# Taking the mixing stage's arithmetic off GpSimd in a one-core decoder-layer kernel

## The chip, the core and the metric

The kernel runs as one program on one core of a Trainium2 chip. Five engines of that core work side by side, each through its own list of instructions, and wait for each other by semaphores: TensorE (PE; its weight loads are shown apart as PEld) multiplies matrices, VectorE (DVE) and ScalarE (ACT) do elementwise work, GpSimd (POOL) does elementwise work and starts some transfers, SyncE (SP) starts transfers. SBUF is the memory on the core that all of them read, PSUM the one that TensorE writes. The metric is the device time of one execution in microseconds (us). All inputs are float32.

## What is computed

One decoder layer on 512 tokens of width 1024, cut to what the kernel's stages are:

```
h = x + 1/2 * SwiGLU_1(RMSNorm(x))          # width 2816
z = RMSNorm(h) @ w_in                        # q | k,v cmp | k,v slc | k,v win | gates | u
q, kc, ksl, kw = rope(...)
o_nsa = nsa_attention(q, ...)                # 8 heads x 64, 2 groups of keys; three branches:
                                             # compressed, selected, window, summed by gates
o_s5  = s5_mixer(u, ...)                     # 32 groups x 16 channels, complex state of 64:
    x_t = a_bar * x_{t-1} + b * u_t          #   associative scan over the tokens
    y = gelu(Re(c x) + d u);  o_s5 = y * sigmoid(y @ w_glu + b_glu)
h = h + concat(o_nsa, o_s5) @ w_out
h = h + 1/2 * SwiGLU_2(RMSNorm(h))
h = h + sigmoid(RMSNorm(h) @ w_gate) * (p @ w_ple)
out = RMSNorm(h)
```

`compress` in the attention adds a position vector to each of the 32 tokens of a window (the "position sums" below), multiplies the flattened window by a matrix, applies gelu and multiplies again.

## The kernel before

Activations lie transposed: 128 features on the partitions, 512 tokens along the row, eight such blocks for width 1024. A product of float32 accuracy is made of three TensorE passes in the rounded type fp32r (`mm3`): the rounded weight `hi` times the rounded input, `hi` times the input's remainder, and the weight's remainder `lo` times the rounded input. Weights come in units of 128 x 1024 (`unit`, L129): one DMA into one of four `raw` buffers, started from ScalarE's queue; `hi` made by ScalarE (L142); `lo = raw - hi` (L143) made by VectorE, or by GpSimd where the caller passes `sub=G`. There are three buffers each of `hi` and `lo`.

The layer goes through FFN 1, the mixing stage (about 385 to 651 us of the profile, its first weight units some 20 us earlier), FFN 2, the embedding gate and the last norm. In the mixing stage:

- the projections (`proj`, L580) make keys, queries, S5 inputs `ut` and compressed keys. Rotated keys and queries and `ut` go out to DRAM and come back in another layout (`kd` and `kf`, `qd` and `qf`, `ud` and `u`, `kcd` and `cst`), by transfers that SyncE starts;
- `s5_all` works in eight chunks of four groups: TensorE makes the drive, VectorE turns it by a rotation (L638 to L641), scans (L644), and turns the state back: two products with the sine on half the partitions each (L647, L648, tile `t`), one with the cosine (L649), and their sum (L652, `xx`);
- `scores` prepares each block of 128 queries (`QA`, `QB`, L883 to L889; rows 64 to 111 of `QB` are zeroed and later hold shift rows, L964) and makes row maxima (L905) and exponentials (L593) of the scores;
- `windows` makes the position sums (L780), `cmp_all` the compressed keys and values with a gelu between its two products, `glu` the S5 outputs: gelu (L596 to L602), a product, a tanh, `sg` (L846), and the split of the result into `oh` and `ol` (L849, L850);
- `out_half` adds the half of the output projection that takes the S5 outputs, column block by column block (L864), and the values of the attention follow, with the other half at the end.

A scheduler sets the order of the instructions on each engine from the program's text and its own estimate of the times; `weave` interleaves the S5 chunks, the scores and the remaining projections in the text. Each engine then works strictly in its order: an instruction that waits holds everything behind it on its engine.

Of the kernel before, what the change touches and what calls it, by code (L numbers as in the profile page):

```python
# [10 lines left out]
F32 = mybir.dt.float32  # L11
# [65 lines left out]
def block_kernel(ctx: ExitStack, tc: tile.TileContext, a: dict, out: bass.AP):  # L77
# [48 lines left out]

    unit_i = [0]

    def unit(raw_only=False, keep=None, sub=None, q=nc.scalar):  # L129
        i = unit_i[0]  # L130
        unit_i[0] += 1
        w = UNIT_W[i]
        if i not in raws:
            load_unit(i, q)
        raw = raws.pop(i)
        if raw_only:
            return raw
        pool, n = (keep, 5) if keep else (ring, 3)
        hi = pool.tile([128, UNIT], FR, tag="hi", name="hi", bufs=n)
        lo = pool.tile([128, UNIT], FR, tag="lo", name="lo", bufs=n)  # L140
        for c in ((slice(0, 512), slice(512, w)) if i == 0 else (slice(0, w),)):
            S.copy(hi[:, c], raw[:, c])  # L142
            (sub or V).tensor_tensor(lo[:, c], raw[:, c], hi[:, c].bitcast(F32), OP.subtract)  # L143
        return hi, lo

    def mm3(o, wh, wl, xh, xl, first, last):
# [391 lines left out]
    def mixer(ctx):  # L538
# [39 lines left out]
        V.tensor_copy(KBc[0:64], zero[0:64, 0:1].to_broadcast([64, 160]))  # L578

        def proj(tag="A"):  # L580
            wu = unit(sub=G)
            o = bank(tag)
            for k in range(KT):
                sl = slice(k * 128, (k + 1) * 128)
                mm3(o, wu[0][:, sl], wu[1][:, sl], nm.xh[:, k, :], nm.xl[:, k, :], k == 0, k == KT - 1)
            return o
# [8 lines left out]
        def gelu2(o, x, w, tag):  # L595

            t = tp.tile([128, SEQ], F32, tag=tag, name="gt")[:, :w]
            act(t, x, AF.Square)
            G.tensor_scalar(t, t, 0.044715, 1.0, OP.mult, OP.add)
            V.tensor_tensor(t, t, x, OP.mult)  # L600
            act(t, t, AF.Tanh, scale=math.sqrt(2 / math.pi))
            V.scalar_tensor_tensor(o, t, 1.0, x, OP.add, OP.mult)  # L602


# [25 lines left out]
        def s5_in(j):  # L630
            sc = s5w.tile([128, GC, 512], F32, tag="sc", name="sc", bufs=3)
            G.dma_start(sc, s5d[:, GC * j:GC * j + GC])
            co, si = sc[:, :, 384:448], sc[:, :, 448:512]
            w = bank(TW, (128, GC, 64))
            for g in range(GC):
                mm(w[:, g], sc[:, g, 0:128], u8[:, GC * j + g], True, True)
            t1, t2 = (s5w.tile([128, GC, 64], F32, tag=n, name=n) for n in ("t1", "t2"))
            V.tensor_tensor(t1, w, co, OP.mult)  # L638
            V.tensor_tensor(t2[64:128], w[0:64], si[0:64], OP.mult)
            V.tensor_tensor(t2[0:64], w[64:128], si[64:128], OP.mult)  # L640
            V.tensor_tensor(t1, t1, t2, OP.subtract)  # L641
            vv = s5w.tile([128, GC, 64], F32, tag="vv", name="vv", bufs=1)
            for g in range(GC):
                V.tensor_tensor_scan(vv[:, g], r8[:, GC * j + g:GC * j + g + 1].to_broadcast([128, 64]), t1[:, g],  # L644
                                     0.0, OP.mult, OP.add)
            x1, x2 = (s5w.tile([128, GC, 64], F32, tag=n, name=n) for n in ("t1", "t2"))
            G.tensor_tensor(x2[64:128], vv[0:64], si[0:64], OP.mult)  # L647
            G.tensor_tensor(x2[0:64], vv[64:128], si[64:128], OP.mult)  # L648
            V.tensor_tensor(x1, vv, co, OP.mult)  # L649
            xx = s5w.tile([128, GC, 64], F32, tag="xx", name="xx")  # L650
            G.memset(xx[:, :, 0:1], 0.0)
            V.tensor_tensor(xx[:, :, 1:64], x1[:, :, 0:63], x2[:, :, 0:63], OP.add)  # L652
            return sc, xx
# [90 lines left out]


        def v_gates():
            wv = [unit(sub=G) for _ in range(3)]
            for b in range(4):
                o = bank("A")
                ov = o[:, :280]  # L750
                for k in range(KT):
                    wt = wv[k // 3]
                    sl = slice((k % 3) * 280, (k % 3) * 280 + 280)
                    xs = slice(b * 128, (b + 1) * 128)
                    mm(ov, nm.xh[:, k, xs], wt[0][:, sl], k == 0, False)
                    mm(ov, nm.xh[:, k, xs], wt[1][:, sl], False, False)
                    mm(ov, nm.xl[:, k, xs], wt[0][:, sl], False, k == KT - 1)
                r1 = nm.ri[:, b:b + 1]
                pv = o[:, 0:256].rearrange("p (r d) -> p r d", r=4)
                S.activation(VL[:, b, :, 0:64], pv, AF.Copy, scale=r1)  # L760
                V.scalar_tensor_tensor(VL[:, b, :, 64:128], pv, r1, VL[:, b, :, 0:64].bitcast(F32),
                                       OP.mult, OP.subtract)
                V.tensor_scalar(gp1[:, b], o[:, 256:280], r1, -1.0, OP.mult, OP.mult)
                yield
            act(gp1, gp1, AF.Exp)
            V.tensor_scalar(gp1, gp1, 5e35, 1.0, OP.min, OP.add)


        def windows(src, i, dst):
            ev = []  # L770
            for g in range(2):
                st = tp.tile([128, SEQ], F32, tag=f"r{g + 1}", name="cst")
                nc.sync.dma_start(st[0:64], src[:, g])
                nc.sync.dma_start(st[64:128, 0:SEQ - 1], src[:, g, 1:SEQ])
                ev.append(st.rearrange("p (j l r) -> p l j r", l=8, r=2)[:, :, :, 0])
            sp = []
            for half, t in enumerate(dst):
                t = t.rearrange("p (l g j) -> p l g j", l=8, g=2)
                for g in range(2):
                    G.tensor_tensor(t[:, :, g], ev[g],  # L780
                                    pe[:, i, 8 * half:8 * half + 8, None].to_broadcast([128, 8, 32]), OP.add)
                sp.append(t)
            return sp
# [42 lines left out]
        def glu():  # L826

            for m in range(4):
                yt = yts[m]
                gelu2(yt, yt, SEQ, ("r1", "r2")[m % 2])  # L830
                S.activation(oh[:, m], yt, AF.Copy, scale=0.5)
                V.scalar_tensor_tensor(ol[:, m], yt, 0.5, oh[:, m].bitcast(F32), OP.mult, OP.subtract)
            yield
            for m in range(4):
                if m % 2 == 0:
                    wu = unit(sub=G)
                o = bank("A")
                for k in range(4):
                    q = (m * 4 + k) % 8
                    sl = slice(q * 128, (q + 1) * 128)  # L840
                    mm3(o, wu[0][:, sl], wu[1][:, sl], oh[:, k], ol[:, k], k == 0, k == 3)
                sg = mp.tile([128, 8, 64], F32, tag="ut", name="sg", bufs=2)
                act(sg.rearrange("p t c -> p (t c)"), o, AF.Tanh, scale=0.5, bias=bglu[:, m:m + 1])
                yf = mp.tile([128, 8, 64], F32, tag="ra", name="yf", bufs=2)
                G.tensor_tensor(yf.rearrange("p t c -> p (t c)"), oh[:, m].bitcast(F32), ol[:, m].bitcast(F32), OP.add)
                V.scalar_tensor_tensor(sg, sg, 1.0, yf, OP.add, OP.mult)  # L846
                nat = sg.rearrange("p t c -> p c t")
                hv_ = oh[:, 4 + m].rearrange("p (c t) -> p c t", t=8)
                S.activation(hv_, nat, AF.Copy, scale=0.5)  # L849
                V.scalar_tensor_tensor(ol[:, 4 + m].rearrange("p (c t) -> p c t", t=8), nat, 0.5, hv_.bitcast(F32),  # L850
                                       OP.mult, OP.subtract)
                yield

        def out_half(ks, done=None, sub=None):
            n = len(ks)
            for m in range(KT):
                o = bank("A")
                for j, k in enumerate(ks):
                    q = (m * n + j) % 8
                    if q == 0:  # L860
                        wu = unit(sub=sub)
                    sl = slice(q * 128, (q + 1) * 128)
                    mm3(o, wu[0][:, sl], wu[1][:, sl], oh[:, k], ol[:, k], j == 0, j == n - 1)
                V.tensor_tensor(h[:, m], h[:, m], o, OP.add)  # L864
# [7 lines left out]
        def scores(qb, env, pool, tags="B", stage=("ra", "ra")):  # L872
# [5 lines left out]
            for hs, st in zip((slice(0, 4), slice(4, 8)), stage):  # L878
                if st == "ra":
                    qf = mp.tile([128, 4, 128], F32, tag=st, name="qf", bufs=2)  # L880
                else:
# [4 lines left out]
                V.tensor_scalar(QB[0:64, hs], qf[0:64], 0.125, None, OP.mult)  # L886
                V.scalar_tensor_tensor(QA[64:128, hs], qf[64:128], 0.125, QA[64:128, hs].bitcast(F32),
                                       OP.mult, OP.subtract)
            G.tensor_copy(QB[64:112].rearrange("p h q -> p (h q)"), zero[64:112, 0:1].to_broadcast([48, 1024]))  # L889
            env.update(QA=QA, QB=QB)  # L890
            yield

# [160 lines left out]
        drain(cg)  # L1053
        drain(gg)
        cc = tp.tile([128, SEQ], FR, tag="rb1", name="cc")[:, :192].rearrange("p (q a c) -> p q a c", q=4, a=2)
        fill = out_half(range(4, 8), sub=G)
        drain(compressed(3, 2))
        shifts(2, 4)
        sg = chain(s1, compressed(1), s0, compressed(0))
# [254 lines left out]
```

## Time and profile before

| | before |
|---|---|
| median of 3 runs | 1113.75 us (1112.89 to 1115.28) |
| profiled execution | 1112.43 us, of which span 1110.6 us |
| PE busy | 1063.3 us, 96% |
| DVE busy | 670.7 us, 60% |
| ACT busy | 389.0 us, 35% |
| POOL busy | 246.5 us, 22% |
| chain that ended last | PE 83%, DVE 5%, DMA 5% |

Busy times are unions, so overlapping ends of one engine's instructions count once. The chain of waits is followed back from the last instruction; what is on it set the end. In the windows view a stretch of the span is taken by itself: the busy time of each engine in it, with the count of instructions, the clock that TensorE was granted there (1.00 is 2.4 GHz, 0.5 is 1.2 GHz) and the DMA engines' share. In the views of waits, an engine's idle time is put down to what came last among the things it waited for.

### The profile page before, as it was taken

To read this page: it belongs to the slowest core of one execution; us is meant where nothing else is said; L and a number is where in the kernel's file an instruction comes from. 1 tells how busy PE (TensorE), PEld (TensorE's weight loads), DVE (VectorE), ACT (ScalarE), POOL (GpSimd) and SP (SyncE) were. 2 spreads that over 40 slices of the span, in tenths; PEclk is the share of its full clock that TensorE was granted. 3 is DMA by queue.
4 is the path that set the end of the run, shared out by engine and by line. 5 is a ranking of instruction groups with operands and counts; after the bars stand their busy time and mean duration, and the time that the engine had idled before them with its cause. 6 is when DMAs were issued, how large, how long until landed. Compare 5 with 4: busy or idle time off the path is not lost.

```text
span 1110.6 us, 13320 instructions
## 1 busy us (share of the span) xinstructions
PE 1063.3 (96%) x5134; PEld 865.4 (78%) x5134; DVE 670.7 (60%) x1129; ACT 389.0 (35%) x636; POOL 246.5 (22%) x245
## 2 busy tenths in 40 slices
PE   7999999999999998898889999999999999999995
PEld 5888888888888886676667578888888888888795
DVE  6995446445448645587777975644454445356755
ACT  6222222123123413256648864221222222224631
POOL 4006146335538533455300000000000000000000
PEclk9999999999999999998899999999999999999998
DMA  7332225327625736667011003233333322232402
GB/s 254 111 114 95 95 95 152 114 95 163 173 101 146 247 114 170 188 203 236 23 58 39 1 21 96 92 105 95 104 95 95 95 95 94 96 95 95 132 1 76
DMA packets 46283, 124.16 MB, mean 112 GB/s; under 512 B 10044, under 2 KB 16796, under 8 KB 45196
## 3 DMA queue, kind: packets, MB, share of 16 engines
q10 hardware_dynamic: 26352, 91.04, 25.4%
q0 software_dynamic: 4336, 17.60, 6.1%
q1 hardware_dynamic: 15532, 14.68, 4.5%
q8 instruction: 40, 0.66, 0.2%
q14 instruction: 23, 0.19, 0.0%
HBM read 109.90 MB, written 13.63 MB: 111 GB/s over the span
## 4 chain that ended last, share of the span: by engine, by line
PE 83%; DVE 5%; DMA 5%; issue 3%; ACT 2%; SPq 1%; POOL 0%; POOLq 0%; DVEq 0%; ACTq 0%
PE ps_A L124 29%; PE ps_B L124 26%; PE ps_C L124 25%; PE ps_D L124 3%; DMA kf<-kd 1%; DMA kd<-r 1%; DMA kcd<-ra 1%; DMA qd<-r 1%; DVE nmax L905 1%; ACT e L593 1%; DVE ol L850 0%; ACT eh L593 0%; ACT ps_B L593 0%; DVE sg L846 0%; DMA raw<-in_wpack 0%
## 5 line engine op out<-in xcount | busy, mean ns | idle before, releaser
L142 ACT CAST hi<-raw 128x1024 fp32r<-128x1024 f32 (+2 forms) x168 | 174.9, 1043 | 540.8 <-PE ps_C L124 184.4
L143 DVE TENSOR_TENSOR lo<-raw,hi 128x1024 fp32r<-128x1024 f32 (+1 forms) x147 | 191.1, 1303 | 75.3 <-ACT hi L142 75.0
L124 PE MATMUL ps_A<-xh,hi 128*128 128x512 f32 (+1 forms) x448 | 170.3, 380 | 7.8 <-ACT xh L164 6.7
L124 PE MATMUL ps_A<-xl,hi 128*128 128x512 f32 (+1 forms) x448 | 169.7, 379 | 0.1
L124 PE MATMUL ps_A<-xh,lo 128*128 128x512 f32 (+1 forms) x448 | 168.9, 377 | 0.8 <-DVE lo L143 0.8
L124 PE MATMUL ps_B<-xh,lo 128*128 128x512 f32 (+1 forms) x432 | 161.9, 375 | 1.2 <-POOL lo L143 1.2
L124 PE MATMUL ps_B<-xl,hi 128*128 128x512 f32 (+1 forms) x432 | 161.8, 374 | 0.0
L124 PE MATMUL ps_B<-xh,hi 128*128 128x512 f32 (+1 forms) x432 | 161.4, 374 | 0.0
L124 PE MATMUL ps_C<-hh,hi 128*128 128x512 f32 x352 | 136.9, 390 | 0.7 <-DVE h L254 0.7
L124 PE MATMUL ps_C<-hl,hi 128*128 128x512 f32 x352 | 137.0, 389 | 0.0
L124 PE MATMUL ps_C<-hh,lo 128*128 128x512 f32 x352 | 136.9, 389 | 0.0
L193 POOL TENSOR_TENSOR ri<-ms,negh 128x4 f32<-128x4 f32 (+1 forms) x6 | 6.5, 1077 | 540.3 <-DVE ms L192 540.3
L124 PEld LDWEIGHTS ps_A<-xh,hi 128*128 128x128 f32 x448 | 85.3, 190 | 24.0 <-ACT xh L164 6.7
L124 PEld LDWEIGHTS ps_A<-xl,hi 128*128 128x128 f32 x448 | 85.3, 190 | 16.6 <-DVE xl L165 1.3
L124 PEld LDWEIGHTS ps_A<-xh,lo 128*128 128x128 f32 x448 | 85.4, 191 | 16.3 <-DVE lo L143 1.0
L232 DVE TENSOR_TENSOR t<-ps_B,rb 128x512 f32<-128x512 f32 x42 | 29.0, 690 | 111.9 <-PE ps_B L124 111.7
L124 PEld LDWEIGHTS ps_B<-xh,lo 128*128 128x128 f32 x432 | 81.1, 188 | 16.4 <-POOL lo L143 1.7
L124 PEld LDWEIGHTS ps_B<-xl,hi 128*128 128x128 f32 x432 | 81.2, 188 | 14.7 <-issue 0.2
L124 PEld LDWEIGHTS ps_B<-xh,hi 128*128 128x128 f32 x432 | 81.2, 188 | 14.5 <-issue 0.2
L254 DVE SCALAR_TENSOR_TENSOR h<-ps_C,h 128x512 f32<-128x512 f32 x64 | 43.9, 689 | 67.0 <-PE ps_C L124 66.9
L124 PEld LDWEIGHTS ps_C<-hh,hi 128*128 128x128 f32 x352 | 66.1, 188 | 15.2 <-DVE h L254 1.5
L124 PEld LDWEIGHTS ps_C<-hh,lo 128*128 128x128 f32 x352 | 66.1, 188 | 13.7
(361 smaller groups left out, 1664.4 us busy)
## 6 DMA issues: line engine op xcount, KB each, us to landing
raw<-in_wpack ACTq DMA_DIRECT2D x168, 512.0 KB, 3.6
sc<-s5d POOLq DMA_DIRECT2D x8, 1024.0 KB, 6.6
raw<-in_wpack SPq DMA_DIRECT2D x4, 512.0 KB, 8.3
h<-in_xT SPq DMA_DIRECT2D x8, 256.0 KB, 4.8
s5d<-fs POOLq DMA_DIRECT2D x1, 2048.0 KB, 11.8
s5d<-gt POOLq DMA_DIRECT2D x1, 2048.0 KB, 12.5
s5d<-tcs POOLq DMA_DIRECT2D x2, 1024.0 KB, 9.5
qf<-qd SPq DMA_DIRECT2D x16, 128.0 KB, 3.7
```

What stands on the lines that cost most here:

```text
L124: PE.matmul(o, lhsT, rhs, start=start, stop=stop, **kw)
L142: S.copy(hi[:, c], raw[:, c])
L143: (sub or V).tensor_tensor(lo[:, c], raw[:, c], hi[:, c].bitcast(F32), OP.subtract)
L193: G.tensor_tensor(ri, ms, negh[:, :nb], OP.pow)
L232: V.tensor_tensor(t3, z[1], nrm.rb, OP.mult)
L254: V.scalar_tensor_tensor(h[:, m, :], o, 0.5, h[:, m, :], OP.mult, OP.add)
L593: S.activation(*args, **kw)
L905: V.tensor_reduce(mc, s_, AX.X, OP.max, negate=True)
```

## The change

No instruction of the mixing stage computes on GpSimd any longer, apart from its memsets, a scaling of a 128 x 4 tile and the power in the norm. Six edits:

1. 21 `lo` subtractions (18 of 1024 columns, two of 840, one of 560) go from GpSimd to VectorE; the `sub` argument is gone.
2. The two sine products of each of the eight S5 chunks (L647, L648, 64 x 256) go to VectorE.
3. The eight position sums (L780, 128 x 256) go to VectorE.
4. The four zeroings of `QB`'s rows (L889, 48 x 1024) go to ScalarE.
5. gelu's middle: the GpSimd operation `t = 0.044715 t + 1` and the VectorE product by `x` become one VectorE operation, `(t + 1/0.044715) x`, with the factor moved into the tanh's scale. Five times.
6. glu: the sum `yf = oh + ol` on GpSimd (L845, four times) is gone; `sg` is multiplied by `yts[m]`, which is twice that sum, and the factor 0.5 becomes 0.25. The tile `sg` takes the buffers ("ra") that `yf` had.

```diff
--- before.py
+++ after.py
@@ -126,7 +126,7 @@
-    def unit(raw_only=False, keep=None, sub=None, q=nc.scalar):
+    def unit(raw_only=False, keep=None, q=nc.scalar):
@@ -140,7 +140,7 @@
             S.copy(hi[:, c], raw[:, c])
-            (sub or V).tensor_tensor(lo[:, c], raw[:, c], hi[:, c].bitcast(F32), OP.subtract)
+            V.tensor_tensor(lo[:, c], raw[:, c], hi[:, c].bitcast(F32), OP.subtract)
         return hi, lo
@@ -578,7 +578,7 @@
-            wu = unit(sub=G)
+            wu = unit()
@@ -596,9 +596,8 @@
             act(t, x, AF.Square)
-            G.tensor_scalar(t, t, 0.044715, 1.0, OP.mult, OP.add)
-            V.tensor_tensor(t, t, x, OP.mult)
-            act(t, t, AF.Tanh, scale=math.sqrt(2 / math.pi))
+            V.scalar_tensor_tensor(t, t, 1 / 0.044715, x, OP.add, OP.mult)
+            act(t, t, AF.Tanh, scale=math.sqrt(2 / math.pi) * 0.044715)
             V.scalar_tensor_tensor(o, t, 1.0, x, OP.add, OP.mult)
@@ -644,8 +643,8 @@
             x1, x2 = (s5w.tile([128, GC, 64], F32, tag=n, name=n) for n in ("t1", "t2"))
-            G.tensor_tensor(x2[64:128], vv[0:64], si[0:64], OP.mult)
-            G.tensor_tensor(x2[0:64], vv[64:128], si[64:128], OP.mult)
+            V.tensor_tensor(x2[64:128], vv[0:64], si[0:64], OP.mult)
+            V.tensor_tensor(x2[0:64], vv[64:128], si[64:128], OP.mult)
             V.tensor_tensor(x1, vv, co, OP.mult)
@@ -777,7 +776,7 @@
                 for g in range(2):
-                    G.tensor_tensor(t[:, :, g], ev[g],
+                    V.tensor_tensor(t[:, :, g], ev[g],
                                     pe[:, i, 8 * half:8 * half + 8, None].to_broadcast([128, 8, 32]), OP.add)
@@ -833,32 +832,31 @@
                 if m % 2 == 0:
-                    wu = unit(sub=G)
+                    wu = unit()
                 o = bank("A")
...
                     mm3(o, wu[0][:, sl], wu[1][:, sl], oh[:, k], ol[:, k], k == 0, k == 3)
-                sg = mp.tile([128, 8, 64], F32, tag="ut", name="sg", bufs=2)
+                sg = mp.tile([128, 8, 64], F32, tag="ra", name="sg", bufs=2)
                 act(sg.rearrange("p t c -> p (t c)"), o, AF.Tanh, scale=0.5, bias=bglu[:, m:m + 1])
-                yf = mp.tile([128, 8, 64], F32, tag="ra", name="yf", bufs=2)
-                G.tensor_tensor(yf.rearrange("p t c -> p (t c)"), oh[:, m].bitcast(F32), ol[:, m].bitcast(F32), OP.add)
+                yf = yts[m].rearrange("p (t c) -> p t c", t=8)
                 V.scalar_tensor_tensor(sg, sg, 1.0, yf, OP.add, OP.mult)
...
                 hv_ = oh[:, 4 + m].rearrange("p (c t) -> p c t", t=8)
-                S.activation(hv_, nat, AF.Copy, scale=0.5)
-                V.scalar_tensor_tensor(ol[:, 4 + m].rearrange("p (c t) -> p c t", t=8), nat, 0.5, hv_.bitcast(F32),
+                S.activation(hv_, nat, AF.Copy, scale=0.25)
+                V.scalar_tensor_tensor(ol[:, 4 + m].rearrange("p (c t) -> p c t", t=8), nat, 0.25, hv_.bitcast(F32),
                                        OP.mult, OP.subtract)
...
 
-        def out_half(ks, done=None, sub=None):
+        def out_half(ks, done=None):
             n = len(ks)
...
                     if q == 0:
-                        wu = unit(sub=sub)
+                        wu = unit()
                     sl = slice(q * 128, (q + 1) * 128)
@@ -886,7 +884,7 @@
                                        OP.mult, OP.subtract)
-            G.tensor_copy(QB[64:112].rearrange("p h q -> p (h q)"), zero[64:112, 0:1].to_broadcast([48, 1024]))
+            S.copy(QB[64:112].rearrange("p h q -> p (h q)"), zero[64:112, 0:1].to_broadcast([48, 1024]))
             env.update(QA=QA, QB=QB)
@@ -1053,7 +1051,7 @@
         cc = tp.tile([128, SEQ], FR, tag="rb1", name="cc")[:, :192].rearrange("p (q a c) -> p q a c", q=4, a=2)
-        fill = out_half(range(4, 8), sub=G)
+        fill = out_half(range(4, 8))
         drain(compressed(3, 2))
```

The three units of `v_gates` (L747) lose their `sub=G` in the same way.

The scheduler reorders around this. Line numbers after the change are one or two lower. The places follow at which the order matters most; tile names carry the number of their buffer.

The first place is VectorE in the projections, in the order before: `ut` are the S5 inputs, `KB` the remainders of the keys that came back from DRAM.

```order
L609 TENSOR_TENSOR ut_3282<-ps_A_3257,rb_3110 128x64x8
L609 TENSOR_TENSOR ut_3316<-ps_D_3291,rb_3110 128x64x8
L722 TENSOR_TENSOR KB_3009<-kf_3157,KA_3008 64x512
L722 TENSOR_TENSOR KB_3009<-kf_3162,KA_3008 64x512
L609 TENSOR_TENSOR ut_3358<-ps_A_3333,rb_3110 128x64x8
L722 TENSOR_TENSOR KB_3009<-kf_3167,KA_3008 64x512
L722 TENSOR_TENSOR KB_3009<-kf_3172,KA_3008 64x512
L609 TENSOR_TENSOR ut_3392<-ps_D_3367,rb_3110 128x64x8
L705 TENSOR_TENSOR r1_3465<-ps_B_3409,cosr_3048 128x512
L706 TENSOR_TENSOR r2_3467<-ps_B_3409,sinr_3049 128x512
```

In the order after the change, the same stretch:

```order
L608 TENSOR_TENSOR ut_3282<-ps_A_3257,rb_3110 128x64x8
L608 TENSOR_TENSOR ut_3316<-ps_D_3291,rb_3110 128x64x8
L143 TENSOR_TENSOR lo_3406<-raw_3403,hi_3405 128x1024
L721 TENSOR_TENSOR KB_3009<-kf_3157,KA_3008 64x512
L721 TENSOR_TENSOR KB_3009<-kf_3162,KA_3008 64x512
L608 TENSOR_TENSOR ut_3358<-ps_A_3333,rb_3110 128x64x8
L143 TENSOR_TENSOR lo_3437<-raw_3434,hi_3436 128x1024
L721 TENSOR_TENSOR KB_3009<-kf_3167,KA_3008 64x512
L721 TENSOR_TENSOR KB_3009<-kf_3172,KA_3008 64x512
L608 TENSOR_TENSOR ut_3392<-ps_D_3367,rb_3110 128x64x8
L143 TENSOR_TENSOR lo_3522<-raw_3519,hi_3521 128x1024
L704 TENSOR_TENSOR r1_3465<-ps_B_3409,cosr_3048 128x512
```

The subtractions `lo_3406` to `lo_3630`, which had GpSimd's order to themselves, now stand between these; `lo_3437` stands behind `ut_3358`.

The second place is VectorE where the shift rows are written into `QB_3505`, the first of the blocks of queries whose values follow, in the order before: `h_66` is the residual, to which each column block of the output projection (`ps_A`) is added.

```order
L905 TENSOR_REDUCE nmax_3055<-ps_B_4702 128x2
L864 TENSOR_TENSOR h_66<-h_66,ps_A_5195 128x512
L143 TENSOR_TENSOR lo_5549<-raw_5546,hi_5548 128x1024
L905 TENSOR_REDUCE nmax_3055<-ps_B_4723 128x2
L964 TENSOR_TENSOR QB_3505<-ps_D_4578,sel_3023 48x1024
L864 TENSOR_TENSOR h_66<-h_66,ps_A_5341 128x512
L905 TENSOR_REDUCE nmax_3055<-ps_B_4757 128x2
```

After the change:

```order
L862 TENSOR_TENSOR h_66<-h_66,ps_A_5478 128x512
L903 TENSOR_REDUCE nmax_3055<-ps_B_4710 128x2
L143 TENSOR_TENSOR lo_5581<-raw_5578,hi_5580 128x1024
L903 TENSOR_REDUCE nmax_3055<-ps_B_4744 128x2
L962 TENSOR_TENSOR QB_3505<-ps_D_4565,sel_3023 48x1024
L862 TENSOR_TENSOR h_66<-h_66,ps_A_5492 128x512
L903 TENSOR_REDUCE nmax_3055<-ps_B_4799 128x2
L862 TENSOR_TENSOR h_66<-h_66,ps_A_5512 128x512
L143 TENSOR_TENSOR lo_5625<-raw_5622,hi_5624 128x1024
L903 TENSOR_REDUCE nmax_3055<-ps_B_4831 128x2
```

In the order before, four additions to `h_66` stand ahead of `QB_3505` in all, and in the order after it six; all but two of the first half's eight are done by then.

The third place is ScalarE around the block of queries `QA_4325` and the compressed keys `KAc`, in the order before; lines L593 are exponentials of scores (`ps_B`) and the tanh and squares of gelu (`gt`).

```order
L885 ACTIVATE QA_4325<-qf_4327 128x512
L885 ACTIVATE QA_4325<-qf_4333 128x512
L806 ACTIVATE chid_4397<-ps_C_4394 128x256
L593 ACTIVATE gt_4379<-yt_4234 128x512
L593 ACTIVATE ps_B_4038,den_3056<-ps_B_4038,nmax_3055 128x384
L106 DMA raw_5546<-in_wpack 128x1024
L814 CAST KAc_3012<-ps_D_4399 64x2x31
L815 CAST KAc_3012<-ps_D_4399 64x2x31
L822 CAST VLc_3011<-ps_D_4406 31x64
L593 ACTIVATE ps_B_4072,den_3056<-ps_B_4072,nmax_3055 128x384
```

After the change:

```order
L883 ACTIVATE QA_4325<-qf_4327 128x512
L883 ACTIVATE QA_4325<-qf_4333 128x512
L887 CAST QB_4326<-zero_3036 48x1024
L593 ACTIVATE ps_B_4100,den_3056<-ps_B_4100,nmax_3055 128x384
L887 CAST QB_4341<-zero_3036 48x1024
L813 CAST KAc_3012<-ps_D_4394 64x2x31
L814 CAST KAc_3012<-ps_D_4394 64x2x31
L593 ACTIVATE gt_4376<-yt_4234 128x512
```

The two zeroings of `QB_4326` and `QB_4341` stand in between now.

## Rows read from the trace of the kernel before

**Rows 1.** Windows: busy of PE, PEld, DVE, ACT, POOL; clock; DMA share; GB/s.

```profile
360.00:385.00 25.00, 25.00 (x112) 20.71 (x111) 18.80 (x25) 11.35 (x16) 12.67 (x15) 1.00 0.87 281
...
515.00:540.00 25.00, 18.91 (x82) 12.71 (x81) 18.74 (x30) 15.96 (x45) 10.36 (x7) 0.75 0.34 107
...
577.00:651.00 74.00, 69.70 (x325) 48.21 (x324) 62.13 (x127) 59.95 (x146) 0.00 (x0) 1.00 0.06 20
...
464.80:576.80 112.00, 97.63 (x602) 72.94 (x602) 90.31 (x179) 62.17 (x150) 47.65 (x49) 0.91 0.43 138
```

**Rows 2.** Waits of TensorE, 416 to 577 us: total us, times, longest.

```profile
PE ps_A L124 <- DVE h L864: 4.2, 1, 4.2
...
PE ps_C L124 <- DMA ud<-ut: 4.1, 1, 4.1
...
PE ps_B L124 <- ACT ps_B L593: 3.4, 5, 1.2
...
PE ps_C L804 <- DVE ht L602: 2.0, 1, 2.0
...
PE ps_B L124 <- POOL lo L143: 1.2, 1, 1.2
```

**Rows 3.** The timeline, GpSimd and VectorE near 561 us: start, length, engine, line.

```profile
560.94 2.34 POOL L143 TENSOR_TENSOR lo<-raw,hi 128x1024 fp32r<-128x1024 f32 x1 [5.22 <-ACT hi L142]
...
561.09 2.23 DVE L943 TENSOR_SCALAR lw<-lw 128x48 int32<-128x48 int32 x1
```

**Rows 4.** Groups of VectorE, 464.8 to 576.8 us: busy us, mean ns, idle.

```profile
L850 DVE SCALAR_TENSOR_TENSOR ol<-sg,oh 128x512 fp32r<-128x512 f32 x4 | 6.6, 1649 | 1.1 <-ACT oh L849 1.1
...
L602 DVE SCALAR_TENSOR_TENSOR yt<-gt,yt 128x512 f32<-128x512 f32 x4 | 5.1, 1283 | 0.0
...
L846 DVE SCALAR_TENSOR_TENSOR sg<-sg,yf 128x512 f32<-128x512 f32 x4 | 4.8, 1198 | 2.3 <-ACT sg L593 2.3
...
L886 DVE TENSOR_SCALAR QB<-qf 64x512 fp32r<-64x512 f32 x5 | 4.5, 921 | 1.7 <-DMA qf<-qd 1.7
...
L832 DVE SCALAR_TENSOR_TENSOR ol<-yt,oh 128x512 fp32r<-128x512 f32 x4 | 4.1, 1034 | 0.3 <-ACT oh L831 0.3
...
L649 DVE TENSOR_TENSOR t<-vv,sc 128x256 f32<-128x256 f32 x7 | 3.1, 443 | 0.0
...
L143 DVE TENSOR_TENSOR lo<-raw,hi 128x1024 fp32r<-128x1024 f32 x1 | 1.2, 1218 | 0.0
```

**Rows 5.** Source view of three such lines: shortest, median, longest ns.

```profile
L850 DVE SCALAR_TENSOR_TENSOR ol<-sg,oh x4: 1069/1159/3209, 544.9 to 557.4; 128x512 fp32r<-128x512 f32 x4
...
L886 DVE TENSOR_SCALAR QB<-qf x5: 408/419/2118, 471.6 to 530.4; 64x512 fp32r<-64x512 f32 x5
...
L832 DVE SCALAR_TENSOR_TENSOR ol<-yt,oh x4: 667/688/2094, 499.5 to 537.9; 128x512 fp32r<-128x512 f32 x4
```

**Rows 6.** The waits of VectorE from 464.8 to 576.8 us.

```profile
DVE nmax L905 <- PE ps_B L124: 7.7, 7, 3.6
...
DVE xx L652 <- POOL t L648: 2.7, 2, 2.1
...
DVE h L864 <- PE ps_A L124: 1.9, 1, 1.9
...
DVE gt L600 <- POOL gt L599: 1.0, 2, 0.5
```

**Rows 7.** The page's fifth part, the cast on ScalarE.

```profile
L142 ACT CAST hi<-raw 128x1024 fp32r<-128x1024 f32 (+2 forms) x168 | 174.9, 1043 | 540.8 <-PE ps_C L124 184.4
```

**Rows 8.** The timeline, VectorE and TensorE, from 431 to 440 us.

```profile
431.06 1.09 DVE L609 TENSOR_TENSOR ut<-ps_A,rb 128x512 f32<-128x512 f32 x1 [6.23 <-DMA ud<-ut]
...
434.17 1.06 DVE L609 TENSOR_TENSOR ut<-ps_D,rb 128x512 f32<-128x512 f32 x1
...
434.72 0.39 PE L124 MATMUL ps_B<-xh,lo 128*128 128x512 f32 x1
...
439.16 1.94 PE L124 MATMUL ps_C<-u,sc 128*128 128x64 f32 x8 [4.05 <-DMA ud<-ut]
```

More of the change, by code (lines that the diff above doesn't have):

```diff
@@ L746, in v_gates @@
         def v_gates():
-            wv = [unit(sub=G) for _ in range(3)]
+            wv = [unit() for _ in range(3)]
             for b in range(4):
```

## Prediction

> **What bounds the kernel now.** I read the page first: TensorE is 96% busy and most of the chain that set the end. So only TensorE's idle time, and time at a lower clock, can be won. The windows view shows where that is [rows 1]. In 360 to 385 us TensorE is busy without a gap while VectorE has 18.80 of 25 us of work and GpSimd 12.67. From 464.8 us (the first score maxima) to 576.8 (the shift rows go into `QB_3505`) it is busy 97.63 of 112.0 us at a granted clock of 0.91, so about 14.4 us idle and some more at the half clock (0.75 in 515 to 540). After that, to 651 us, GpSimd does nothing; TensorE is busy 69.70 of 74.00 us, VectorE 62.13, ScalarE 59.95.
>
> TensorE's waits in 416 to 577 us come next [rows 2]: 4.2 us for one addition to the residual on VectorE, 4.1 for the S5 inputs' way through DRAM, 3.4 for ScalarE's exponentials in five pieces, 2.0 for gelu's last operation on VectorE; of those put down to GpSimd's `lo` the larger is 1.2. So GpSimd is hardly waited for directly. The timeline shows how it matters all the same [rows 3]: at 561.09 VectorE's operation on a 128x48 tile takes 2.23 us and ends 0.04 us after GpSimd's `lo` (560.94, 2.34 us). The lines of such a group have ordinary and very long members, 667 to 2094 ns at L832, 408 to 2118 at L886, 1069 to 3209 at L850 [rows 5], the long ones beside GpSimd's operations. So GpSimd's work costs VectorE time, and VectorE is what TensorE waits for.
>
> **The change part by part.** The sum is made in four stretches, against the profiled execution of 1112.43 us.
>
> *To 416 us: 0.* Three of the `lo` move between FFN 1's last operations on VectorE, 3 x 1.22 [rows 4] = 3.7 us, where 6.2 us of 25 are idle and TensorE has no gap [rows 1]; that idle time is the cover. Without it they cost at most these 3.7. A zeroing of `QB` on ScalarE (nearest: the cast of 128x1024, 1.04 us [rows 7]) lies beside 13.65 us of idle time there.
>
> *416 to 464.8 us: +0.4.* Seven subtractions leave GpSimd (2.34 us for one of 1024 columns [rows 3]) and take 1.22 on VectorE [rows 4], but stand in its order now. `lo_3437` is behind `ut_3358`, which VectorE could start only at 431.06, for a transfer, and which takes 1.09 [rows 8]. So it runs from about 432.1 to 433.3. It is used in the third of 24 matmuls whose last started at 434.72; at one in 25.00/112 = 0.223 us [rows 1] the third was due at 430.0, and is due at 428.8 once the 1.2 us for `lo_3406` [rows 2] is not lost: a new wait of 4.5. Its 21 remaining steps of 0.223 us end at about 438.4. In the trace TensorE stood still there until 439.16, for the S5 inputs [rows 8], so the new wait lies within the old one of 1.2 and the 4.1 us. What counts is the transfer: it starts with `ut_3392` (434.17), which has `lo_3437` and two `KB` of 0.6 ahead of it (KB and `ut` both queue behind the waiting instruction) and starts at about 434.6: +0.4. Bounds: -2.3 (if what VectorE loses today beside GpSimd at its `KB` starts all transfers earlier by as much), and +3 (if two more subtractions of 1.22 get ahead of `ut_3392` and the new wait outlasts the old).
>
> *464.8 to 576.8 us: -1.7.* VectorE's 90.31 us there hold time in which it only stood still. Each line's count times what its mean is above its shortest: L850 4 x 0.58, L602 4 x 0.60 (the shortest as at L832, 0.68), L846 4 x 0.52, L886 5 x 0.51, L832 4 x 0.37, and 2.0 at L943 for an operation that I take at 0.2: 12.8 us [rows 3 to 5]. This goes. What comes, at durations of the same stretch [rows 4]: 14 sine products (0.44, as 128x256 at L649) 6.2, eight position sums (0.44) 3.5, seven `lo` 8.5 and the narrow one 0.7, and, since they stand ahead of `QB_3505` now, two residual additions and one maximum of 128x512 (0.68 each) 2.0: 20.9. So 90.3 - 12.8 + 20.9 = 98.4 us of work. The folded gelu costs VectorE nothing, one operation for one. Before, VectorE idled 21.7 us. The waits for GpSimd go (2.7 + 1.0); so do the one for the addition (1.9) and about half of the longest for TensorE (3.6 [rows 6]), which followed the 2.0 us wait for gelu; and added work fills some 2 us of the rest. That leaves 12: 110.4 us in place of 112.0, or, with rounding, -1.7. Bounds: VectorE 95% busy (103.5 us, -8.5), or idle as long as before (120.1, +8.1). I take a value nearer to the low idle, since more work in the same queue fills gaps. The two zeroings on ScalarE near 520 us stand ahead of exponentials that TensorE waits for; ScalarE is busy only 15.96 of 25 us there [rows 1], so I take 0, bound 2 x 1.04 = +2.1.
>
> By the Trainium skill, Perfetto Trace Analysis, section "Optimizing Scalar/DVE Operations", work may be offloaded from a saturated VectorE to ScalarE or even GpSimd, with the doubt that the shared port may leave nothing won between VectorE and GpSimd. By its first half this change goes the wrong way, as VectorE comes to 98.4 of some 110 us (89%); by its second half the 12.8 us are the price of the offloading. The rows bear out the second half (12.8 us lost on VectorE for 20.9 us saved there) and also the first, as a balance of 8 us is left against the change.
>
> *576.8 to 651 us: -3.3.* At `QB_3505` TensorE has done two more column blocks of the output projection, 24 matmuls at 0.223 us, 5.4, and a small group of scores: some 6 us less is left for the stretch after. With TensorE at 94% there, nearly all of it would count; with VectorE at 84% and ScalarE at 81% as second and third limit I take little more than half. Bounds: 0 and -6.
>
> The removal of `yf` shortens a chain on GpSimd that VectorE had no long wait for: 0, covered by VectorE's other work.
>
> Sum: 0 + 0.4 - 1.7 - 3.3 = -4.6, so 1112.43 becomes 1107.8. The profiled execution lies 1.3 us under the median of the runs shown; put on top, this gives 1109.1: I predict 1109.
>
> **The rivals.** *A, VectorE becomes the bound.* Between 464.8 and 576.8 us VectorE keeps its old idle time, because its operations stand in a fixed order among the waits for TensorE's scores, for ScalarE and for transfers, and each `lo` now stands behind one of these, with TensorE waiting for the `lo`. It decides from an idle time of 16.5 us on: 98.4 + 16.5 = 114.9 is +2.9, which uses up the 0.4 - 3.3 of the other stretches. At 21.7 us of idle it is +8.1, in all +5.2: 1119. For it: VectorE's busiest stretch gets busier, and TensorE's longest waits [rows 2] are for VectorE, not GpSimd. Against it: 3.7 of the 21.7 us were waits for GpSimd itself.
>
> *B, the stalls go altogether.* VectorE at 95% (-8.5), the front -2.3, the last stretch -6: -16.8, so 1097. For it: TensorE's idle time and half clock in the middle hold more than that [rows 1], and the waits for the addition and for gelu's end (4.2, 2.0) follow held-up operations. Against: 3.4 us of waits are for ScalarE, and the transfers stay.
>
> *C, no change.* The round trips through DRAM hold the front, and what VectorE gains by not standing still it spends on the new work: within 2 us, 1112 to 1116. For it: 12.8 against 20.9 us, close to a balance after the idle time.
>
> **How the numbers follow.** Forecast 0.42, A 0.28, B 0.13, C 0.17. The range is 1099 to 1120; it takes in A's point and most of B's, and leaves out A's and B's ends. The forecast's own range is 1105 to 1113, by half of its bounds on either side. About 0.2%, or 2.2 us, is what a measurement of this kernel can tell from no change. Of the forecast 0.37 lies more than that under 1113.75 and 0.05 within; with B that is 0.50 faster. C and a little of A (0.04) make it 0.26 within. The rest of A, 0.24, is slower.
>
> **What would show it.** Right: no VectorE operation of 128x512 over 1.3 us in 416 to 577; VectorE's busy time from its first score maximum to `QB_3505` near 98 us and its stretch near 110; a wait of TensorE of 4 to 5 us for a VectorE `lo` near 429; the wait of 4.2 for the addition gone or under 2; the stretch after `QB_3505` some 3 us shorter. Wrong: waits of TensorE for VectorE's `lo` or maxima of over 10 us in all in the middle (A); VectorE without gaps there and the clock near 1.00 (B); the late operations on VectorE as long as before, which would mean that not GpSimd held them up.

## The result, and the profile after

| | before | after |
|---|---|---|
| median | 1114.85 us, 8 runs | 1108.61 us, 8 runs |
| profiled span | 1110.6 us | 1104.2 us |
| PE busy | 1063.3 us | 1059.0 us |
| DVE busy | 670.7 us | 681.7 us |
| ACT busy | 389.0 us | 393.4 us |
| POOL busy | 246.5 us | 164.4 us |

The ratio of after to before is 0.9934, 95% interval 0.9913 to 0.9955: 0.66% faster, 6.2 us by the medians. The forecast was 1109, from a sum of -4.6 us; the spans of the profiled executions differ by 6.4. Of these 6.4 us, 4.3 are TensorE's busy time, for the same 5134 matmuls, and 2.1 its idle time (47.3 to 45.2). The windows view of after, its middle stretch bounded by the same instructions as in [rows 1]:

```profile
360.00:385.00 25.00, 25.00 (x112) 20.71 (x111) 18.67 (x28) 12.40 (x17) 4.62 (x11) 1.00 0.82 279
...
515.00:540.00 25.00, 17.29 (x88) 11.18 (x86) 19.02 (x44) 16.31 (x42) 0.00 (x0) 0.71 0.14 42
...
463.80:578.20 114.40, 102.75 (x637) 77.25 (x637) 96.98 (x216) 66.59 (x157) 2.67 (x9) 0.91 0.41 138
...
578.20:650.80 72.60, 69.16 (x321) 47.88 (x320) 61.80 (x128) 59.08 (x144) 0.00 (x0) 1.00 0.04 14
```

The middle (from the product `ra`, L740, just ahead of the first score maxima, to the end of the write into `QB_3505`) takes 114.4 us, 2.4 more than before, and TensorE does 637 matmuls in it in place of 602. The stretch behind it takes 72.6 us up to the end of the first addition of the last half's column blocks. In before that stretch was 79.6 us long:

```profile
576.80:656.40 79.60, 75.30 (x350) 52.58 (x348) 64.56 (x132) 60.94 (x148) 0.00 (x0) 1.00 0.06 19
```

TensorE's waits from 416 to 577 us in after, against [rows 2]:

```profile
PE ps_B L124 <- DVE QA L885: 5.1, 1, 5.1
...
PE ps_B L124 <- DVE lo L143: 4.1, 1, 4.1
...
PE ps_B L124 <- ACT ps_B L593: 3.5, 3, 2.3
...
PE ps_A L124 <- ACT oh L830: 2.9, 2, 2.7
...
PE ps_A L124 <- DVE h L862: 0.6, 1, 0.6
```

The wait for the residual addition fell from 4.2 to 0.6 us, and the wait for the S5 inputs (4.1) and for GpSimd's `lo` are gone. In their place stand 5.1 us for VectorE's `QA` and 4.1 for its `lo`, both ahead of the middle stretch; behind the first is a transfer, as VectorE itself stood until 460.53 for `qf`, which `QA` is made from. The lines that had long members beside GpSimd's operations [rows 5], in the source view of after (shortest, median, longest ns):

```profile
L848 DVE SCALAR_TENSOR_TENSOR ol<-sg,oh x4: 1060/1092/1119, 547.4 to 556.2; 128x512 fp32r<-128x512 f32 x4
...
L884 DVE TENSOR_SCALAR QB<-qf x5: 408/411/419, 470.8 to 535.5; 64x512 fp32r<-64x512 f32 x5
...
L831 DVE SCALAR_TENSOR_TENSOR ol<-yt,oh x4: 678/682/692, 493.7 to 540.5; 128x512 fp32r<-128x512 f32 x4
```

No member is long any more. VectorE's own waits in the middle stretch, against [rows 6]:

```profile
DVE nmax L903 <- PE ps_B L124: 4.8, 5, 2.3
...
DVE QB L884 <- DMA qf<-qd: 3.3, 2, 2.2
...
DVE ol L848 <- ACT oh L847: 1.9, 3, 1.2
...
DVE cosr L779 <- DMA cst<-vcd: 1.5, 1, 1.5
```

Those for GpSimd are gone; one for a transfer (`qf`) has grown from 1.7 to 3.3 us, and one is new: the position sums (L779) have brought their own wait for a transfer, 1.5 us, into VectorE's order.

### The profile page after: what moved, and what is told of

Same layout as the page of the kernel before. It is cut to its first block, busy times and chain, and to the rows that moved or that the text cites. A ratio compares the mean times of both kernels' runs of the same rounds, so it can differ in the third digit from the quotient of the medians.

```text
span 1104.2 us, 13275 instructions
## 1 busy us (share of the span) xinstructions
PE 1059.0 (96%) x5134; PEld 862.7 (78%) x5134; DVE 681.7 (62%) x1174; ACT 393.4 (36%) x640; POOL 164.4 (15%) x187
## 4 chain that ended last, share of the span: by engine, by line
PE 79%; DVE 8%; DMA 5%; ACT 4%; issue 4%; SPq 0%; POOLq 0%; ACTq 0%; POOL 0%; DVEq 0%
PE ps_A L124 27%; PE ps_B L124 25%; PE ps_C L124 25%; PE ps_D L124 2%; DMA kf<-kd 1%; DVE nmax L903 1%; DMA kd<-r 1%; DVE lo L143 1%; DMA qf<-qd 1%; ACT e L593 1%; DMA qd<-r 1%; ACT eh L593 1%; ACT ps_B L593 1%; DMA cst<-vcd 0%; DVE vv L643 0%
## 5 line engine op out<-in xcount | busy, mean ns | idle before, releaser
L143 DVE TENSOR_TENSOR lo<-raw,hi 128x1024 fp32r<-128x1024 f32 (+2 forms) x168 | 215.4, 1284 | 85.8 <-ACT hi L142 85.3
```

Of the source, the lines that this page charges most:

```text
L143: V.tensor_tensor(lo[:, c], raw[:, c], hi[:, c].bitcast(F32), OP.subtract)
```

## The experiments

The theory T: GpSimd's operations that read SBUF hold VectorE's up; taking them off GpSimd frees more of VectorE's time than the moved work takes. The rivals: R1, the gain is the new order of the program alone; R2, the gain is the two operations folded away. All ratios are to the kernel before on the same chip, with a 95% interval.

**1. GpSimd's work put beside VectorE again, in the same order.** In the changed kernel GpSimd makes six of the subtractions a second time, into `raw`, which nobody reads afterwards (the code is cut).

```diff
             V.tensor_tensor(lo[:, c], raw[:, c], hi[:, c].bitcast(F32), OP.subtract)
+            if dup:    # glu's two units, four units of the output projection
+                G.tensor_tensor(raw[:, c], raw[:, c], hi[:, c].bitcast(F32), OP.subtract)
```

> The changed kernel, with GpSimd doing six subtractions a second time: behind VectorE's `lo` of glu's two units and of the four units of the first half of the output projection, GpSimd writes raw - hi back into `raw`, which nobody reads. The orders of TensorE and VectorE are word for word those of the changed kernel. T: six operations of 2.4 us that read SBUF come back beside VectorE; each holds it up by about 1.5 us, in the stretch where it is the bound: 3 to 7 us over the changed kernel, ratio to before 0.996 to 1.000, with VectorE operations of 2 us or more in the trace again. R1 (the order alone is the gain): within 1 us of the changed kernel, ratio 0.993 to 0.994.

Measured: 1.0018 (1.0002 to 1.0033), 0.84% over the changed kernel's 0.9934; the span is 9.8 us longer, more than T expected. The timeline of this kernel, VectorE and GpSimd (start, length, engine, line):

```profile
510.00 0.68 DVE L905 TENSOR_REDUCE nmax<-ps_B 128x1 f32<-128x512 f32 x1
...
510.60 1.77 DVE L642 TENSOR_TENSOR t<-t,t 128x256 f32<-128x256 f32 x1
...
514.36 2.91 DVE L645 TENSOR_TENSOR_SCAN vv<-r,t 128x64 f32<-128x64 f32 x4
...
509.71 2.37 POOL L145 TENSOR_TENSOR raw<-raw,hi 128x1024 f32<-128x1024 f32 x1 [1.66 <-DMA raw<-in_wpack]
...
514.18 2.40 POOL L145 TENSOR_TENSOR raw<-raw,hi 128x1024 f32<-128x1024 f32 x1 [2.10 <-DVE lo L143]
```

and the same two VectorE operations in the changed kernel:

```profile
509.95 0.41 DVE L640 TENSOR_TENSOR t<-t,t 128x256 f32<-128x256 f32 x1
...
512.35 0.83 DVE L643 TENSOR_TENSOR_SCAN vv<-r,t 128x64 f32<-128x64 f32 x4
```

A subtraction of 0.41 us takes 1.77, four scans of 0.83 take 2.91; both groups end 0.3 and 0.7 us after GpSimd's operation beside them (509.71 + 2.37 and 514.18 + 2.40). The maximum at 510.00, read from PSUM, isn't held. TensorE's and VectorE's orders are the same in both kernels, so R1 can't explain the difference. Each of the six holds one operation up, by 0.8 to 2.1 us, and VectorE's busy time grows by 9.2 us (681.7 to 690.9) for the same 1174 instructions; TensorE's waits for `lo` don't grow (4.6 and 4.3 us). The six cost 9.8 us of the span, 1.6 each: 6.2 us are TensorE's idle time, 3.6 its busy time, with a granted clock of 0.981 over the span against 0.984. T's mechanism is shown, and its price in this order; that the time won pays for the work that VectorE takes over is not.

**2. The subtractions alone.**

```diff
-            (sub or V).tensor_tensor(lo[:, c], raw[:, c], hi[:, c].bitcast(F32), OP.subtract)
+            V.tensor_tensor(lo[:, c], raw[:, c], hi[:, c].bitcast(F32), OP.subtract)
```

> The kernel before with one of the six edits: all 21 subtractions `lo` go from GpSimd to VectorE; the sine products, position sums, zero rows, gelu and `yf` stay as before. Theory T (GpSimd's operations that read SBUF hold VectorE's up, and that lost time pays for the work VectorE takes over): the subtractions are the longest of GpSimd's operations, so most of the gain is here: 3 to 6 us under before, ratio 0.995 to 0.997, and no VectorE operation of 128x512 over 1.5 us beside a GpSimd one in glu. Rival R2 (the gain comes from the two operations taken out of gelu and glu): no change, within 2 us. Rival R1 (the gain comes from the new order, which does two column blocks of the output projection earlier): nothing definite, since the order is a third one.

Measured: 1.0011 (0.9996 to 1.0027). No gain: T's number was wrong. TensorE's waits from 405 to 580 us, and a windows row:

```profile
PE ps_B L124 <- ACT ps_B L593: 9.2, 8, 2.6
...
PE ps_B L124 <- DVE lo L143: 4.5, 1, 4.5
...
PE ps_A L124 <- ACT hi L142: 2.9, 1, 2.9
```

```profile
416.00:640.00 224.00, 199.93 (x1063) 151.09 (x1061) 169.69 (x337) 122.00 (x283) 35.59 (x47) 0.89 0.36 114
```

The wait for `lo` behind `ut_3358` is there as forecast, and TensorE waits 9.2 us for ScalarE's exponentials (3.4 before). VectorE's busy time grows by 9.1 us over the span (670.7 to 679.8), so what GpSimd's subtractions held up there doesn't pay for what VectorE takes over. But TensorE is idle 1.9 us less than before in all (45.4 us); its busy time is 5.7 us longer, for the same matmuls, at a granted clock of 0.89 in this stretch against 0.94 before. So in this run it is the clock, and not more idle time, that took the gain.

**3. The subtractions put back.** `sub=G` again for all 21 in the changed kernel.

> The changed kernel with the 21 subtractions `lo` put back on GpSimd, the other five edits kept. T: it gives back most of the gain: 0 to 3 us under before, ratio 0.997 to 1.000. R2: it keeps most, 5 us under before, ratio 0.995.

Measured: 1.0000 (0.9980 to 1.0020), as T expected and against R2. TensorE's longest waits there:

```profile
PE ps_D L124 <- DVE xx L651: 7.4, 2, 6.6
...
PE ps_D L124 <- DVE VLc L822: 3.2, 1, 3.2
```

The first, 6.6 us of it in one piece, is for the sum `xx` of an S5 chunk. The small moves have brought its two sine products into VectorE's queue (0.42 us each), and GpSimd's `lo` holds its scans up (1.98 us in place of 0.82); that is some 2 us of the 6.6; the rest is not explained.

**4. The folds alone.** In before, edits 5 and 6.

```diff
-            G.tensor_scalar(t, t, 0.044715, 1.0, OP.mult, OP.add)
-            V.tensor_tensor(t, t, x, OP.mult)
+            V.scalar_tensor_tensor(t, t, 1 / 0.044715, x, OP.add, OP.mult)
...
-                G.tensor_tensor(yf.rearrange("p t c -> p (t c)"), oh[:, m].bitcast(F32), ol[:, m].bitcast(F32), OP.add)
+                yf = yts[m].rearrange("p (t c) -> p t c", t=8)
```

> The kernel before with the two folded operations alone (gelu's middle in one VectorE operation, `yf` gone); nothing is moved from one engine to another. T: little, 0 to 2 us under before, ratio 0.998 to 1.000, since 5 + 4 of GpSimd's operations are gone but its long ones stay. R2: most of the gain, 5 us or more, ratio 0.995.

Measured: 0.9890 (0.9871 to 0.9908), 1102.39 us in four runs: better than the whole change. R2 was right on this run and T wrong. VectorE is still held up by GpSimd's subtractions there (source view, shortest, median, longest ns):

```profile
L844 DVE SCALAR_TENSOR_TENSOR sg<-sg,yt x4: 693/1544/2407, 537.4 to 546.2; 128x512 f32<-128x512 f32 x4
...
L831 DVE SCALAR_TENSOR_TENSOR ol<-yt,oh x4: 671/688/1877, 503.8 to 534.8; 128x512 fp32r<-128x512 f32 x4
```

**5 and 6. Each fold by itself.**

> The kernel before with gelu's folded operation alone (five GpSimd operations fewer, VectorE's count unchanged; `yf`, the subtractions, sine products, position sums and zero rows stay). Both folds together took 1.1% off, ratio 0.989. F1 (gelu's hop through GpSimd, in the chain square, GpSimd, VectorE, tanh, is what cost): most of that, ratio 0.988 to 0.992. F2 (the sums `yf` on GpSimd, 1.3 to 2.0 us each beside glu's VectorE operations, cost): ratio 0.998 to 1.000. The order of TensorE differs from that with both folds in only 22 rows.

> The kernel before with `yf` taken out alone (four GpSimd operations of 128x512 fewer); gelu as before. F1: little, ratio 0.998 to 1.000. F2: most of the 1.1%, ratio 0.989 to 0.992.

Measured: gelu's fold 0.9920 (0.9902 to 0.9937), `yf` 1.0015 (0.9999 to 1.0031). So F1, as far as it goes: gelu's fold, not the sum `yf`. Two windows of gelu's fold, to be set beside before and after above (515 to 540) and below (416 to 640):

```profile
515.00:540.00 25.00, 20.74 (x113) 14.99 (x112) 21.46 (x31) 19.01 (x45) 15.90 (x10) 1.00 0.43 128
...
416.00:640.00 224.00, 200.88 (x1116) 148.40 (x1115) 175.40 (x346) 132.75 (x310) 61.17 (x55) 0.98 0.38 114
```

The granted clock is 1.00 where before has 0.75 and after 0.71, and 0.98 over the long stretch where before has 0.94. TensorE's busy time over the whole span is 1058.5 us against 1063.3: that is 4.8 of the 7.4 us by which the spans differ (1103.2 and 1110.6).

**7. The hop without the fold.** gelu's GpSimd operation made by VectorE (`G.tensor_scalar` becomes `V.tensor_scalar`).

> The kernel before with gelu's GpSimd operation made by VectorE, unfolded: five GpSimd operations fewer, five VectorE operations more. The hop is gone, the VectorE operation is not. F1: most of the gain of gelu's fold, ratio 0.990 to 0.994. If the gain of that fold is a lucky order of the scheduler and not the hop: near 1.000, since its order is another one.

Measured: 0.9981 (0.9965 to 0.9998), nearer to what was expected of a lucky order than to F1. Five operations more add 1.8 us to VectorE's busy time (669.9 in gelu's fold, 671.7 here), and the medians are 8.5 us apart (1113.66 and 1105.18), so most of that is not their own time. TensorE's order is another one too, and two waits stand out, with ScalarE's timeline at the first:

```profile
PE ps_B L124 <- ACT ps_B L593: 9.3, 5, 7.6
...
PE ps_A L124 <- DVE ol L832: 4.2, 1, 4.2
```

```profile
476.98 0.63 ACT L885 ACTIVATE QA<-qf 128x512 fp32r<-128x512 f32 x1 [10.30 <-DMA qf<-qd]
...
477.52 0.64 ACT L593 ACTIVATE ps_B<-ps_B,nmax 128x512 f32<-128x512 f32 x1
```

One of 7.6 us for a single exponential, and one of 4.2 for `ol`, are not in gelu's fold. The exponential stands behind `QA` on ScalarE, which waited 10.30 us for a transfer: the order put it there, not the operation. So this run doesn't tell the hop from the order.

**8. Folds and subtractions.**

> Both folds, and all 21 subtractions `lo` on VectorE; sine products, position sums and zero rows on GpSimd. Against the changed kernel it lacks the three smaller moves. If each move costs by itself (work added to VectorE's queue): between the folds alone and the changed kernel, ratio 0.990 to 0.993. If the long subtractions are worth moving once the folds are in: under the folds alone, ratio 0.985 to 0.988.

Measured: 0.9957 (0.9944 to 0.9970), above both ranges expected: the subtractions, moved on top of the folds, lose 0.67%; moved on top of the folds and the small moves (3 against the changed kernel) they gain 0.66%. The edits don't add up.

**9 to 11. The same instructions in another order.** `S1 = 34` becomes `S1 = 33`, a number in `weave`, in before, in the changed kernel and in the folds alone.

> The kernel before with one number of the weave changed (S1 from 34 to 33, the steps over which the scores are spread): every instruction is the same, the scheduler's order is another one in the mixing stage (316 rows of TensorE's order differ). O (the order that the scheduler happens to find decides some 5 us, and part of what the single edits gain or lose is that): ratio off 1.000 by 0.003 or more to either side. W (the work on each engine decides, the order does not): 0.998 to 1.002.

> The changed kernel with the same number changed. W: 0.992 to 0.995, as the changed kernel. O: outside of that by 0.003 or more.

> The kernel with the two folds alone, with the same number changed. W: 0.987 to 0.991, as with S1 at 34. O: outside of that by 0.003 or more; if it comes near 1.000, the folds' 1.1% was mostly a fortunate order.

Measured: before 0.9997 (0.9985 to 1.0009), changed 0.9983 (0.9968 to 0.9997), folds 0.9947 (0.9925 to 0.9968). Before doesn't care; the other two lose 0.5 and 0.6% with no instruction added. O holds for them. The windows view from 416 to 640 us shows it in TensorE's matmuls (the count behind its busy time), for before, changed, folds, then changed and folds with S1 at 33:

```profile
416.00:640.00 224.00, 198.61 (x1082) 147.81 (x1081) 169.14 (x332) 125.48 (x295) 64.90 (x60) 0.94 0.38 114
```

```profile
416.00:640.00 224.00, 200.82 (x1106) 149.68 (x1105) 181.82 (x378) 133.21 (x307) 3.39 (x11) 0.94 0.36 114
```

```profile
416.00:640.00 224.00, 203.64 (x1112) 151.79 (x1111) 172.58 (x345) 132.20 (x308) 54.22 (x51) 0.95 0.38 114
```

```profile
416.00:640.00 224.00, 201.31 (x1092) 150.47 (x1092) 179.94 (x373) 130.88 (x300) 3.40 (x11) 0.92 0.36 114
```

```profile
416.00:640.00 224.00, 201.25 (x1082) 148.41 (x1081) 166.33 (x334) 126.31 (x296) 54.78 (x51) 0.93 0.37 114
```

In the same 224 us TensorE gets through 1082, 1106 and 1112 matmuls, but only 1092 and 1082 in the other orders (a rough measure, as they are of unlike size). The granted clock is 0.94 to 0.95 in the first three and 0.92 to 0.93 in the last two. In the changed kernel TensorE is idle alike in both orders (23.2 and 22.7 us of the 224), so what the order took there is clock; in the folds the idle time grows as well (20.4 to 22.8). All runs together agree: the mean of their granted clocks over the span is 0.988 for the folds and 0.983 with S1 at 33, 0.981 and 0.978 for the changed kernel, 0.980 and 0.979 for before.

**12. A version of the best parts.** The folds, and of the subtractions only those of glu and of the output projection on VectorE.

> Both folds, and of the 21 subtractions the six of glu and of the first half of the output projection on VectorE, the fifteen of the projections on GpSimd; sine products, position sums and zero rows on GpSimd. T (GpSimd's operations hold VectorE up where VectorE is the bound, and cost nothing where it has idle time): the best of all, ratio 0.983 to 0.988. If the moved subtractions cost VectorE what the held ones did: 0.989 to 0.993.

Measured: 0.9939 (0.9923 to 0.9955), above both ranges expected and not the best. The version that beats both kernels is 4, in the one order that the scheduler found for it; in its other order (11) it is level with the change.

## Why the prediction was right, and where it was not

The time, 1108.61 against 1109, and its sign came out, and its mechanism, that GpSimd's operations hold VectorE's up, was right. Of the terms of the sum each of the three that aren't 0 was off, by 1.4 to 4.1 us and not in the same direction; that the sum still came to -4.6 where the spans gave -6.4 is in part luck.

*What bounds the kernel, and GpSimd's hold on VectorE*: right. The long members are gone, and VectorE's work in the middle came to 96.98 us where the forecast had 98.4. Experiment 1 shows the mechanism with the order held.

*416 to 464.8 us, +0.4*: it ended 1.0 us earlier. The new wait of TensorE for `lo_3437` was forecast at 4.5 us near 429 and is 4.12, inside the old wait for the S5 inputs, as said. The timeline of after, VectorE and TensorE:

```profile
430.30 1.03 DVE L608 TENSOR_TENSOR ut<-ps_A,rb 128x512 f32<-128x512 f32 x1 [7.82 <-DMA ud<-ut]
...
431.18 1.21 DVE L143 TENSOR_TENSOR lo<-raw,hi 128x1024 fp32r<-128x1024 f32 x1
...
433.50 1.04 DVE L608 TENSOR_TENSOR ut<-ps_D,rb 128x512 f32<-128x512 f32 x1
...
432.44 0.50 PE L124 MATMUL ps_B<-xh,lo 128*128 128x512 f32 x1 [4.12 <-DVE lo L143]
...
438.98 0.39 PE L124 MATMUL ps_B<-xh,lo 128*128 128x512 f32 x1
...
439.21 1.00 PE L124 MATMUL ps_C<-u,sc 128*128 128x64 f32 x8
```

The three starts at 430.30, 431.18 and 433.50 are the S5 inputs, `lo_3437` and the next inputs; TensorE goes on at 432.44 and has the inputs' chunk right behind its last matmul, without waiting. These came 0.8 to 1.1 us earlier than forecast, beginning with `ut_3358`. That is not where the 1.0 us comes from, though: TensorE begins the inputs' chunk at 439.21, and began it at 439.16 before [rows 8]. Its eight matmuls then take 1.00 us in place of 1.94, at a granted clock of 1.00 from 440 to 460 us against 0.86; but a wait for `QA` of 5.1 us (1.4 before), which the forecast did not have, follows. By the end of this stretch TensorE has done 7 matmuls fewer than before (2052 and 2059), so the border has moved here too, and the 1.0 us is no gain by itself.

*464.8 to 576.8 us, -1.7*: +2.4. The term that failed is VectorE's idle time, taken at 12 us and measured at 17.4 (114.4 - 96.98). The waits for GpSimd went as forecast, but added work filled no gap behind transfers and ScalarE, as rival A had it: VectorE's waits for transfers grew from 1.7 to 4.8 us (`qf` and the new one for `cst`), and those for ScalarE stayed (4.6 and 4.8 us in all). A's point to decide was 16.5 us of idle time, and it was passed; that A did not come about is due to the next term.

*576.8 to 651 us, -3.3*: -7.0. The forecast let little more than half of the moved work count; all of it did. TensorE had 350 matmuls left before and 321 now, 29 fewer; its busy time fell by 6.1 us (75.30 to 69.16) and its idle time by 0.9 (4.3 to 3.4). VectorE and ScalarE, feared as second and third limit, didn't hold it up. The two terms are one: the border between them moved, and together they are -4.6 against -5.0. The first addition of the last half in before and in after:

```profile
655.68 0.69 DVE L864 TENSOR_TENSOR h<-h,ps_A 128x512 f32<-128x512 f32 x1 [1.51 <-PE ps_A L124]
```

```profile
650.12 0.69 DVE L862 TENSOR_TENSOR h<-h,ps_A 128x512 f32<-128x512 f32 x1 [1.51 <-PE ps_A L124]
```

That is 5.6 us earlier; the remaining 0.8 of the spans' 6.4 lie behind this row.

*Edits costed at nothing*: wrong. "The folded gelu costs VectorE nothing" held, but I gave the folds no gain, and alone they give 1.1% in their order and 0.5% in another. `yf`, put at 0, gave nothing. The subtractions, on which I put the freed time, give nothing by themselves (experiment 2), as rival C had it for the whole. That the result is 0.66% and not 0.2% hangs on the order (experiment 10).

*Left open*: why gelu's fold gains. Its gain goes with the granted clock: the mean over the span is 0.987 in its six runs and 0.980 in those of before on the same chip. What keeps the clock up, the missing hop or the order that came with it, isn't shown; no run has the fold and the hop in one order. Nor was it tried whether a GpSimd operation that only writes holds VectorE.

By the Trainium skill, Perfetto Trace Analysis, section "Optimizing Scalar/DVE Operations", moving work between VectorE and GpSimd may win nothing, as they share a port. The ratio for moving the subtractions alone, 1.0011, agrees, though its order and its clock differ too.

## What to carry to other kernels

Before moving work from GpSimd to VectorE, add up what GpSimd's operations hold on VectorE (each line's mean over its shortest member) against what the moved work takes; if they are near each other, look for operations to fold away instead. Where a scheduler makes the order, a gain of half a per cent can be the order's: run the same instructions in a second order before crediting an edit, and compare the granted clock of both. A stretch with a moving border is judged with its neighbour: count what the bounding engine got done in it.

## What the runs showed of the hardware

A GpSimd subtraction of 128x1024 holds up not only VectorE's operations with two large inputs but scans too (0.83 to 2.91 us for four of 128x64, experiment 1) and operations on tiny tiles (2.23 us for 128x48, [rows 3]). In these rows the held operation ended 0.04 to 0.7 us after GpSimd's, however little VectorE had to do in it. The maximum that read PSUM was not held (0.68 us at 510.00, experiment 1).
